# One core of a hybrid RWKV-7 / mLSTM / MoE block: the scheduler of the long stretch plans with mean durations from the trace

## The chip, the cores and the metric

The kernel runs on one core of a Trainium2 chip. The metric is the device time of one execution in microseconds (us). A core has five engines with their own instruction queues: TensorE (PE) for matmuls, VectorE (DVE), ScalarE (ACT), GpSimd (POOL), and SyncE (SP), which here only issues transfers (DMAs). A queue is worked off in order; an instruction whose inputs aren't there holds up all behind it on the same queue.

## What is computed

One block of an encoder on 1024 tokens of width 1024: a modulated RMS norm, one input projection, two groups of recurrent heads on its columns, an output projection, and a hierarchical mixture of experts. All of it is float32.

```python
# RWKV-7 group, 8 heads x 64: u is the projection's columns after the token shift
r, k, v, wd, ad, gd = split(u)
decay = exp(-exp(-softplus(-(w0 + tanh(wd) @ w_up)) - 0.5))
a = sigmoid(a0 + ad @ a_up);  g = sigmoid(gd) @ g_up
kk = normalise(k * k_k);  k = k * (1 + (a - 1) * k_a);  b = kk * a
state = state * decay_t + (state @ -kk_t) b_t + v_t k_t      # for each token t
y_t = state @ r_t                                            # then group norm, bonus, * g
# mLSTM group, 4 heads, qk 64 / v 128, in chunks, gated; then
x = x + gate * (concat(rwkv, mlstm) @ w_out)
x = x + gate * moe(rms_norm(x))        # top-1 of 4 groups, top-2 of 8 experts, 1024 -> 256 -> 1024
```

## The kernel before, in words

A product in full float32 precision is made from three passes of fp32r matmuls: the left and the right side are split into a high and a low part (hTh, hTl for the activations; whi, wlo for the weights), and high x high, low x high and high x low are added up. These matmuls, 128 rows by 512 columns, go into PSUM tiles named lane. A block of weights (wraw, five buffers, half of a 128-column block each) is fetched by SP, its high part is made on ACT, and its low part (wlo) on VectorE for one half and on POOL for the other (fetch_w, split_w).

The RWKV group is worked through in eight units, numbered 0 to 7: four pairs of heads in each half of 512 tokens. A unit has six parts, each a function. unit_prep makes decays, k, kk, AR and BK, mostly on VectorE; unit_rest makes what the scan needs besides; between them the products of AR and BK, masked to tiles G, are formed on TensorE and VectorE. unit_solve inverts 16 x 16 triangles: G is copied to DRAM (dF), read back turned (N), fifteen rounds of a multiplication (Xt) and a sum (XD) follow on VectorE, four writes put XD into DRAM (img), and two reads bring it back as D and X. unit_levels doubles the blocks to 32 and 64 with matmuls of D, G, X and T, beginning with tp<-D,G on TensorE and T<-tp,ll on VectorE. unit_scan goes through the chunks of the state (pr, pu, pp, py in PSUM; R, UV, st). unit_post is group norm, bonus and gate (nrs is its reciprocal square root, Y its result).

Beside the units stand: the remaining modulation vectors (ada_rest, 32 loads ada_w of 512 KB through three buffers, each followed by one scalar_tensor_tensor of 128 x 1024 on VectorE), the normalised input of the second half (xin, with its reciprocal square roots xrs and xss), the mLSTM gates and chunks (qko, vd, pB, rowd, yTd), and the lanes of the input and output projections.

From 63.8 us on the program isn't issued as it is written. A Recorder notes each operation with what it reads and writes (add), its step's priority (PRIO) and an expected duration (cost). flush then plans all of it with a list scheduler: it goes through planned time, and at each point gives every free engine the ready operation of the lowest rank, where rank is 20 x priority minus the longest planned path from the operation to the end (bl), if its tiles have space. The operations are issued in this order, for all five queues, up to 842.1 us. Every one is issued through the same line of add, so the profile puts all of them at L262 (L290 in the changed file). In cost, a matmul goes by its size, a VectorE operation takes 0.13 us + elements / 880, an ACT operation 0.2 + elements / 1350, a POOL operation 0.4 + elements / 610; in add, a DMA moves 300e3 bytes per us one after the other; in flush its result lands 1.7 us after that.

Of the kernel before, what the change touches and what calls it, by code (L numbers as in the profile page):

```python
# [9 lines left out]
F32R = mybir.dt.float32r  # L10
# [39 lines left out]
class View:  # L50
# [90 lines left out]
class Pool:  # L141


    def __init__(self, rec, make):
        self.rec, self.make, self.pool, self.users, self.opened = rec, make, None, [], None
        rec.control(self, True)

    def start(self):
# [42 lines left out]


PRIO = dict(prep=2, rest=3, lev=1, scan=0, post=4, gates=6, ada=9, rx=8, h=3, chunk=5, split=5, prod=7, fin=4, fetch=5, y=4)
PE_SLACK = 0.5
RANK = 20.0


class Recorder:
# [14 lines left out]
    def control(self, pool, begin):  # L213
        if self.mode != 'record':
            pool.start() if begin else pool.end()
            return
        o = Op()
        o.engine, o.what, o.cost, o.pe = 'ctl', None, 0.0, False
# [13 lines left out]
    def cost(self, engine, what, a, kw):  # L232
        free = lambda x: math.prod(x.shape[1:])
        if engine == 'tensor':
            out, w = a[0], a[1]
            n, m = free(out), free(w)
            if what == 'transpose':
                return 0.112
            if isinstance(w, View) and w.base.dtype_ == F32R:
                return 0.231 * max(n, 128) / 512  # L240
            if out.shape[0] <= 32:
                return 0.012 if n <= 32 else 0.05
            return 2 * max(0.112 * m / 128, 0.84e-3 * n, 0.05)
        out = a[0] if a else kw['out']
        n = max([free(x) for x in list(a) + list(kw.values()) if hasattr(x, 'shape')])
        if what.endswith('dma_start'):
            return 0.45
        if engine == 'vector':
            return 0.13 + n / 880.0 * (2 if what == 'tensor_tensor_scan' else 1)
        if engine == 'scalar':  # L250
            return 0.2 + n / 1350.0 + (0.19 if 'accum_out' in kw else 0)
        return 0.1 + n / 1500.0 if what == 'memset' else 0.4 + n / 610.0

    def add(self, engine, what, a, kw):
        o = Op()
        o.engine, o.what, o.pe = engine, what, engine == 'tensor'
        o.cost = self.cost(engine, what, a, kw)
        o.dma = 0.0
        if what.endswith('dma_start'):
            o.dma = 4.0 * math.prod(a[0].shape) / 300e3  # L260
        fn = getattr(self.nc, engine)
        call = lambda: getattr(fn, what)(*[real(x) for x in a], **{k: real(x) for k, x in kw.items()})  # L262
        writes = [a[0]] if a else [kw['out']]
        if 'accum_out' in kw:
            writes.append(kw['accum_out'])
# [3 lines left out]
        for x, w in acc:  # L269
            if isinstance(x, View):  # L270
                key, box = x.base, x.box
# [39 lines left out]
    def flush(self):  # L311
# [23 lines left out]
        free['ctl'] = 0.0  # L335
        dma_free = 0.0
        cand = {e: [] for e in free}
        for o in ops:
            if not o.wait:
                cand[o.engine].append(o)  # L340
        now, left = 0.0, len(ops)
        placed = set(t for s in self.slots.values() for t in s)
        self.plan = []
# [28 lines left out]
        while left:  # L372
            busy = False
            for e in free:
                if free[e] > now:
                    continue
                best = None
                for o in cand[e]:
                    if o.ready <= now:
                        if (best is None or (o.rank, o.seq) < (best.rank, best.seq)) and room(o, now):  # L380
                            best = o
                if best is None:
                    continue
                o = best
                busy = True
                cand[e].remove(o)
                left -= 1
                o.begin = now
                for t in o.tiles:
# [13 lines left out]
                for u in users[o]:  # L403
                    u.wait -= 1
                    lat = 0.0 if u.pe and o.pe else 0.1 if u.engine == o.engine or o.engine == 'ctl' else 0.15 + (PE_SLACK if u.pe else 0.0)
                    u.ready = max(u.ready, o.done + lat if not (u.pe and o.pe) else o.done)
                    if not u.wait:
                        cand[u.engine].append(u)
            if busy:
                continue  # L410
            nxt = [free[e] for e in free if free[e] > now]
# [15 lines left out]
class Block:  # L427
    def __init__(self, ctx, tc, aps):
# [4 lines left out]
        self.dram = ctx.enter_context(self.pool(name="dscr", bufs=1, space=DRAM))  # L433
        self.img = {}
        self.psum = ctx.enter_context(self.pool(name="psum", bufs=1, space=PSUM))

    def pool(self, **kw):
        return Pool(self.rec, lambda: self.tc.tile_pool(**kw))
# [2111 lines left out]
```

## Time and profile before

| | us |
|---|---|
| median of 3 runs | 1303.49 |
| lowest, highest | 1301.4, 1307.46 |
| the profiled execution | 1305.22 |
| its span (first to last instruction) | 1303.3 |
| mean granted TensorE clock, of full | 0.91 |
| the planned stretch | 63.8 to 842.1 |

The page gives busy time, share and count of each engine, then the span in 40 slices. In views by instruction, a row is start, duration, engine, line, operation, output<-inputs, shapes and how many there were in a row; in brackets stands how long the engine idled before and on what it waited. Groups give count, busy time and mean ns of one. SPq is SP's queue. Names lose their buffer numbers, so all eight units have the same ones and are told apart by time.

### The profile page before, as it was taken

How to read it: one execution, taken by the hardware profiler on the slowest of the kernel's cores; microseconds unless marked ns; L12 is line 12 of the kernel's file. 1: busy time of each engine (PE TensorE's matmuls, PEld its weight loads, DVE VectorE, ACT ScalarE, POOL GpSimd, SP SyncE). 2: the span in 40 equal slices, each digit the busy share in tenths (PEclk: the TensorE clock that was granted, in tenths of full speed). 3: DMA queues.
4: the chain of work that ended last, by engine and by line, in shares of the span. 5: the costliest groups of instructions: out<-in, count | busy, mean ns of one | idle time of the engine just before them, and what ended most of it. 6: DMA issues, size and time to landing. Idle time of an engine off the chain costs nothing.

```text
span 1303.3 us, 21771 instructions
## 1 busy us (share of the span) xinstructions
PE 1148.8 (88%) x7807; PEld 836.3 (64%) x7807; DVE 936.3 (72%) x2024; ACT 529.2 (41%) x1021; POOL 393.9 (30%) x464
## 2 busy tenths in 40 slices
PE   3886889797999999999898899995899999898893
PEld 3665666676676777776666677774666666565553
DVE  6699676876656878877748554834688888777766
ACT  5343112142433443333422333644455655455444
POOL 4623134221233242432133323543222222222112
PEclk8887677698999999999899699997799999999997
DMA  9525555475433443322433554699599999999974
GB/s 313 153 69 155 180 174 153 122 204 158 136 96 97 107 112 80 104 69 61 94 119 102 154 159 134 195 361 326 190 306 314 302 289 285 282 320 326 324 264 164
DMA packets 251935, 246.16 MB, mean 189 GB/s; under 512 B 55064, under 2 KB 190362, under 8 KB 251824
## 3 DMA queue, kind: packets, MB, share of 16 engines
q1 hardware_dynamic: 243504, 228.43, 56.2%
q0 software_dynamic: 8320, 16.31, 5.4%
q8 instruction: 62, 1.02, 0.3%
q14 instruction: 49, 0.40, 0.1%
HBM read 212.13 MB, written 44.74 MB: 197 GB/s over the span
## 4 chain that ended last, share of the span: by engine, by line
PE 62%; DMA 16%; DVE 13%; issue 3%; ACT 2%; SPq 1%; POOL 1%; DVEq 0%; ACTq 0%; POOLq 0%
PE lane L262 20%; PE tp L262 14%; PE yd L2049 8%; DMA wd<-in_moe_w_down_dram 4%; PE lane L787 4%; PE lane L788 4%; PE lane L789 3%; DMA ada_w<-in_ada_w_dram 2%; DMA D<-img 2%; DMA wa<-in_moe_w_gate_dram 2%; PE tp L2002 2%; PE lane L189 2%; PE py L262 1%; DMA X<-img 1%; DVE Xt L262 1%
## 5 line engine op out<-in xcount | busy, mean ns | idle before, releaser
L262 PE MATMUL lane<-hTh,whi 128*128 128x512 f32 (+1 forms) x469 | 213.5, 455 | 2.5 <-DVE v L262 0.7
L262 PE MATMUL lane<-hTl,whi 128*128 128x512 f32 (+1 forms) x469 | 192.3, 410 | 5.7 <-DVE hTl L262 5.7
L262 PE MATMUL lane<-hTh,wlo 128*128 128x512 f32 (+1 forms) x469 | 190.8, 407 | 3.1 <-DVE wlo L262 3.1
L262 ACT CAST whi<-wraw 128x512 fp32r<-128x512 f32 (+1 forms) x120 | 71.6, 607 | 163.8 <-PE lane L262 133.8
L2049 PE MATMUL yd<-wd,a 128*112 128x512 f32 x256 | 119.8, 607 | 12.5 <-DMA wd<-in_moe_w_down_dram 9.3
L262 POOL TENSOR_TENSOR wlo<-wraw,whi 128x512 fp32r<-128x512 f32 (+1 forms) x60 | 81.9, 1367 | 97.2 <-ACT whi L262 95.1
L262 PEld LDWEIGHTS lane<-hTh,whi 128*128 128x128 f32 (+1 forms) x469 | 91.0, 194 | 30.9 <-issue 2.2
L262 PEld LDWEIGHTS lane<-hTh,wlo 128*128 128x128 f32 (+1 forms) x469 | 90.9, 194 | 27.2 <-DVE wlo L262 4.8
L262 PEld LDWEIGHTS lane<-hTl,whi 128*128 128x128 f32 (+1 forms) x469 | 91.4, 195 | 20.6 <-DVE hTl L262 8.3
L1972 DVE TENSOR_TENSOR wl<-wa,wh 128x1024 fp32r<-128x1024 f32 x62 | 75.6, 1225 | 40.2 <-ACT wh L1971 38.8
L787 PE MATMUL lane<-wh,xh 128*112 128x512 f32 x256 | 103.9, 406 | 0.0
L788 PE MATMUL lane<-wl,xh 128*112 128x512 f32 x256 | 101.7, 397 | 0.0
L789 PE MATMUL lane<-wh,xl 128*112 128x512 f32 x256 | 100.7, 393 | 0.0
L262 POOL TENSOR_SCALAR sW<-st,WT 128x64 f32<-128x64 f32 x56 | 33.1, 592 | 215.5 <-DVE st L262 129.9
L2076 POOL DMA_INDIRECT x2d<-ys,idx x30 | 44.9, 1496 | 147.4 <-DVE ys L2060 138.5
L2049 PEld LDWEIGHTS yd<-wd,a 128*112 128x112 f32 x256 | 43.5, 182 | 65.4 <-issue 44.6
L1972 DVE TENSOR_TENSOR wl<-wb,wh 128x1024 fp32r<-128x1024 f32 x62 | 76.4, 1233 | 11.3 <-ACT wh L1971 9.6
L1971 ACT CAST wh<-wa 128x1024 fp32r<-128x1024 f32 x62 | 64.8, 1049 | 45.4 <-PE lane L789 36.5
L1971 ACT CAST wh<-wb 128x1024 fp32r<-128x1024 f32 x63 | 66.2, 1051 | 17.4 <-PE lane L789 8.3
L1978 POOL DMA_INDIRECT xt<-xad,idx x32 | 35.0, 1093 | 113.3 <-PE tp L2002 94.9
L262 DVE COPY UV<-pu 64x64 f32<-64x64 f32 x128 | 28.1, 220 | 38.3 <-PE pu L262 36.9
L789 PEld LDWEIGHTS lane<-wh,xl 128*112 128x112 f32 x256 | 44.9, 175 | 14.8 <-DVE xl L2015 0.4
(515 smaller groups left out, 2539.2 us busy)
## 6 DMA issues: line engine op xcount, KB each, us to landing
wd<-in_moe_w_down_dram SPq DMA_DIRECT2D x64, 512.0 KB
wraw<-in_w_in_dram SPq DMA_DIRECT2D x104, 256.0 KB
ada_w<-in_ada_w_dram SPq DMA_DIRECT2D x32, 512.0 KB
wa<-in_moe_w_gate_dram SPq DMA_DIRECT2D x32, 512.0 KB
wa<-in_moe_w_up_dram SPq DMA_DIRECT2D x32, 512.0 KB
wb<-in_moe_w_gate_dram SPq DMA_DIRECT2D x32, 512.0 KB
wb<-in_moe_w_up_dram SPq DMA_DIRECT2D x32, 512.0 KB
ada_w<-in_ada_w_dram SPq DMA_DIRECT2D x32, 256.0 KB
```

What stands on the lines that cost most here:

```text
L189: return getattr(eng, what)(*[real(x) for x in a], **{k: real(x) for k, x in kw.items()})
L262: call = lambda: getattr(fn, what)(*[real(x) for x in a], **{k: real(x) for k, x in kw.items()})
L787: nc.tensor.matmul(ps, l[0], r[0], start=first, stop=False)
L788: nc.tensor.matmul(ps, l[0], r[1], start=False, stop=False)
L789: self.mark = nc.tensor.matmul(ps, l[1], r[0], start=False, stop=last)
L1971: nc.scalar.copy(h, src)
L1972: (engs[n] if engs else nc.vector).tensor_tensor(l, src, h.bitcast(F32), op=ALU.subtract)
L1978: return self.nc.gpsimd.indirect_dma_start(out=self.xts[e % 3], out_offset=None, in_=self.xad[:], in_offset=bass.IndirectOffsetOnAxis(ap=s ...
L2002: self.nc.tensor.transpose(pt[:, j, :], v[:, j // 2, j % 2], self.ident[0:SL, 0:SL])
L2049: self.nc.tensor.matmul(y[:, b], a[:, i], d[:, i, b * 512:b * 512 + 512], start=(i == 0), stop=(i == 1))
L2076: self.nc.gpsimd.indirect_dma_start(out=self.x2d[:], out_offset=bass.IndirectOffsetOnAxis(ap=oi, axis=0), in_=ys, in_offset=None, bounds_c ...
```

## The change

The scheduler gets a table COST of mean durations in us, by engine (g, s, v), operation and the tag of the tile that is written. cost looks there first. What isn't in the table (matmuls, copies on ACT, tensor_reduce, and the tags R, UV, ada_rest among others) keeps the formula. The two DMA constants become 250e3 bytes per us and 2.0 us. The rest of the diff are hooks by which an operation could be put on another engine; other() gives None for all of them, so that alts stays empty.

```diff
+COST = {
...
+    ('v', 'tensor_tensor'): dict(nrs=0.2, wlo=0.85, BK=1.06, k=1.02, lg1=0.66, Xt=0.37, Y=0.76, hTl=0.97, msm=0.24, mrs=0.19),
...
+}
...
         if what.endswith('dma_start'):
             return 0.45
+        known = COST.get((engine[0], what), {}).get(out.base.key[1] if isinstance(out, View) else '')
+        if known:
+            return known
         if engine == 'vector':
...
+    def other(self, engine, what, a, kw):
+        return None
...
         if what.endswith('dma_start'):
-            o.dma = 4.0 * math.prod(a[0].shape) / 300e3
...
+            o.dma = 4.0 * math.prod(a[0].shape) / 250e3
+        o.alt = self.other(engine, what, a, kw)
...
-            o.bl = max((u.bl for u in users[o]), default=0.0) + o.cost + (0.25 if o.engine != 'ctl' else 0.0) + (getattr(o, 'dma', 0) and o.dma + 1.7)
+            o.bl = max((u.bl for u in users[o]), default=0.0) + o.cost + (0.25 if o.engine != 'ctl' else 0.0) + (getattr(o, 'dma', 0) and o.dma + 2.0)
...
-                for o in cand[e]:
+                for o in cand[e] + alts[e]:
                     if o.ready <= now:
-                        if (best is None or (o.rank, o.seq) < (best.rank, best.seq)) and room(o, now):
-                            best = o
+                        k = (o.rank, o.seq)
+                        if (best is None or k < key) and (o.engine == e or sooner(o, now)) and room(o, now):
+                            best, key = o, k
...
-                    o.done = max(dma_free, o.done + o.dma) + 1.7
+                    o.done = max(dma_free, o.done + o.dma) + 2.0
```

Every engine has as many instructions as before, in another order. Three places of it follow. The first is SP's queue in unit 6, from just after the first img write (img_586 is the DRAM image that XD is written to, D the tile that is read back from it). Before:

```order
L262 DMA wraw<-in_w_in_dram 128x4x128
L262 DMA img_586<-XD 16x32x16 x3
L262 DMA wraw<-in_w_in_dram 128x4x128 x2
L262 DMA vd<-vtm 128x4x128
L262 DMA D_6794<-img_586 128x1x256
```

The same place with the change:

```order
L290 DMA gn<-in_rwkv_gn_w_dram 128x128
L290 DMA img_586<-XD 16x32x16 x2
L290 DMA yTd<-yt 128x512
L290 DMA img_586<-XD 16x32x16
L290 DMA D_6761<-img_586 128x1x256
```

The loads of wraw and vd no longer stand between the writes of img and the read of D; the vector gn and yTd stand among the writes.

The second place is VectorE in unit 3, from the last G to the first Xt (N is the turned G, xin and xrs belong to the input of the second half, Y to the group norm of an earlier unit). Before:

```order
L262 TENSOR_TENSOR G_3016<-tp,mask 128x512
L262 TENSOR_TENSOR D_3070<-tp,D_2908 128x256
L262 SCALAR_TENSOR_TENSOR qko<-qks,qko 128x512
L262 STREAM_TRANSPOSE X<-D_3070 32x8x32 x4
L262 COPY bon<-tp 128x8
L262 COPY u_257<-lane 128x3
L262 TENSOR_SCALAR carry<-lane,pcol 128x1
L262 COPY UV_2856<-pu 64x64
L262 COPY UV_2861<-pu 64x64
L262 TENSOR_TENSOR Xt<-N_3119,XD 64x1
```

With the change 41 rows lie between the two; the first nine of them are:

```order
L290 TENSOR_TENSOR G_3279<-tp,mask 128x512
L290 COPY UV_2744<-pu 64x64
L290 COPY UV_2749<-pu 64x64
L290 TENSOR_TENSOR wlo<-wraw,whi 128x512
L290 COPY bon<-tp 128x8
L290 TENSOR_TENSOR Y<-Y,bv 128x512
L290 SCALAR_TENSOR_TENSOR st<-pp,WT,sW 128x64
L290 TENSOR_TENSOR Y<-Y,tp 128x512
L290 TENSOR_TENSOR R<-pr,AV 128x64
L290 COPY UV_2744<-pu 64x64
```

and the last five before the first Xt:

```order
L290 TENSOR_TENSOR xrs<-xrs,xss 128x1
L290 SCALAR_TENSOR_TENSOR xss<-xrs 128x1
L290 SCALAR_TENSOR_TENSOR xrs<-xrs 128x1
L290 TENSOR_SCALAR xin<-xin,xss 128x1024
L290 TENSOR_TENSOR Xt<-N_3381,XD 64x1
```

The four transposes of X went elsewhere, and steps of an earlier unit's scan and group norm and the chains of xrs, xss and xin came in.

The third place is SP's queue in unit 0, from the load of ada_rest's bias to the read of D (three rows of ada_w stand ahead of it in both). Before:

```order
L262 DMA ada_rest<-in_ada_b_dram 1x1024
L262 DMA img_586<-XD 16x32x16 x2
L262 DMA ada_w<-in_ada_w_dram 128x1024 x2
L262 DMA img_586<-XD 16x32x16
L262 DMA ada_w<-in_ada_w_dram 128x1024
L262 DMA img_586<-XD 16x32x16
L262 DMA ada_w<-in_ada_w_dram 128x1024
L262 DMA wraw<-in_w_in_dram 128x4x128 x2
L262 DMA D_1235<-img_586 128x1x256
```

With the change:

```order
L290 DMA ada_rest<-in_ada_b_dram 1x1024
L290 DMA wraw<-in_w_in_dram 128x4x128 x2
L290 DMA ada_w<-in_ada_w_dram 128x1024 x2
L290 DMA img_586<-XD 16x32x16
L290 DMA ada_w<-in_ada_w_dram 128x1024 x2
L290 DMA img_586<-XD 16x32x16
L290 DMA ada_w<-in_ada_w_dram 128x1024
L290 DMA img_586<-XD 16x32x16
L290 DMA ada_w<-in_ada_w_dram 128x1024
L290 DMA img_586<-XD 16x32x16
L290 DMA ada_w<-in_ada_w_dram 128x1024 x2
L290 DMA D_1201<-img_586 128x1x256
```

Eight loads of ada_w stand between the bias and D instead of four.

## Rows read from the trace of the kernel before

**Rows 1.** The page: busy us, share and instructions of each engine.

```profile
PE 1148.8 (88%) x7807; PEld 836.3 (64%) x7807; DVE 936.3 (72%) x2024; ACT 529.2 (41%) x1021; POOL 393.9 (30%) x464
PEclk8887677698999999999899699997799999999997
```

**Rows 2.** Table by stage; columns as its second line names them.

```profile
core 0: us, PE busy (x) PEld busy (x) DVE busy (x) ACT busy (x) POOL busy (x), PEclk, DMA share, GB/s
63.80:303.30 239.50, 197.49 (x1653) 150.47 (x1654) 191.12 (x423) 69.11 (x125) 67.06 (x76) 0.80 0.53 153
303.30:356.00 52.70, 50.71 (x498) 38.58 (x499) 33.42 (x122) 19.08 (x35) 8.35 (x13) 0.93 0.50 142
356.00:495.30 139.30, 133.60 (x1042) 99.07 (x1043) 96.84 (x265) 54.23 (x118) 47.36 (x66) 0.99 0.39 104
495.30:638.00 142.70, 134.46 (x1292) 97.21 (x1291) 112.71 (x312) 48.68 (x100) 42.57 (x64) 0.98 0.31 76
638.00:755.60 117.60, 104.72 (x791) 76.62 (x792) 69.56 (x196) 34.31 (x80) 39.33 (x43) 0.83 0.45 124
755.60:842.10 86.50, 83.41 (x627) 64.42 (x628) 52.50 (x144) 40.15 (x132) 34.78 (x40) 0.95 0.55 160
```

**Rows 3.** Timeline of TensorE, at full clock: start, duration, what.

```profile
223.57 0.39 PE L262 MATMUL lane<-hTh,whi 128*128 128x512 f32 x1
...
224.27 0.39 PE L262 MATMUL lane<-hTh,whi 128*128 128x512 f32 x1
...
397.16 0.66 PE L262 MATMUL tp<-ident,xin 128*128 128x128 f32 x4
397.58 0.50 PE L262 MATMUL lane<-hTh,whi 128*128 128x512 f32 x1
...
399.22 0.34 PE L262 MATMUL pp<-UV,BKT 128*64 128x64 f32 x4
```

**Rows 4.** Groups on VectorE, 67 to 842 us: count, busy us, mean ns, idle before.

```profile
L262 DVE SCALAR_TENSOR_TENSOR ada_rest<-ada_w,csil,ada_rest 128x1024 f32<-128x1024 f32 x32 | 42.4, 1324 | 4.1 <-DMA ada_w<-in_ada_w_dram 4.0
...
L262 DVE SCALAR_TENSOR_TENSOR nrs<-nrs 128x8 f32<-128x8 f32 x80 | 17.0, 229 | 1.1
...
L262 DVE TENSOR_TENSOR BK<-k,Ei 64x512 f32<-64x512 f32 x16 | 14.6, 910 | 0.2
...
L262 DVE TENSOR_TENSOR k<-k,aa 128x512 f32<-128x512 f32 x8 | 8.2, 1022 | 0.0
```

**Rows 5.** Timeline of VectorE in unit 3's chain.

```profile
308.12 0.69 DVE L262 TENSOR_TENSOR G<-tp,mask 128x512 f32<-128x512 f32 x1 [3.10 <-PE tp L262]
...
318.59 0.46 DVE L262 COPY UV<-pu 64x64 f32<-64x64 f32 x2 [3.67 <-PE pu L262]
319.08 0.15 DVE L262 TENSOR_TENSOR Xt<-N,XD 64x1 f32<-64x1 f32 x1
...
331.49 0.38 DVE L262 TENSOR_REDUCE XD<-Xt 64x15 f32<-64x225 f32 x1
...
356.04 0.42 DVE L262 TENSOR_TENSOR T<-tp,ll 128x256 f32<-128x256 f32 x1 [1.32 <-PE tp L262]
```

**Rows 6.** Timeline of SP's queue in unit 6, from the last img writes to D.

```profile
619.12 1.56 SPq L262 DMA_DIRECT2D img<-XD  x3
626.62 3.35 SPq L262 DMA_DIRECT2D wraw<-in_w_in_dram  x2
...
631.02 0.54 SPq L262 DMA_DIRECT2D D<-img  x1
```

**Rows 7.** Timeline of TensorE at the same place.

```profile
636.89 1.08 PE L262 MATMUL tp<-D,G 32*32 32x32 f32 x64 [4.46 <-DMA D<-img]
```

**Rows 8.** Timeline of VectorE: one operation at two times.

```profile
121.14 1.74 DVE L262 TENSOR_TENSOR k<-k,aa 128x512 f32<-128x512 f32 x1
...
247.78 0.68 DVE L262 TENSOR_TENSOR k<-k,aa 128x512 f32<-128x512 f32 x1
```

**Rows 9.** Waits of TensorE, 67 to 842 us: total us, times, longest.

```profile
PE tp L262 <- DMA D<-img: 17.6, 6, 5.8
```

**Rows 10.** Waits of SP's queue, 67 to 842 us.

```profile
SPq L262 <- POOL wlo L262: 70.8, 23, 6.6
```

More of the change, by code (lines that the diff above doesn't have):

```diff
@@ L144, in __init__ @@
     def __init__(self, rec, make):
-        self.rec, self.make, self.pool, self.users, self.opened = rec, make, None, [], None
+        self.rec, self.make, self.pool, self.users, self.opened, self.psum = rec, make, None, [], None, False
         rec.control(self, True)
@@ L193 @@
 PRIO = dict(prep=2, rest=3, lev=1, scan=0, post=4, gates=6, ada=9, rx=8, h=3, chunk=5, split=5, prod=7, fin=4, fetch=5, y=4)
+COST = {
+    ('g', 'memset'): dict(X=0.52, cs=0.52, adr=0.95),
+    ('g', 'tensor_copy'): dict(WT=0.49, XD=0.69),
+    ('g', 'tensor_scalar'): dict(sW=0.59, gd=0.62, qko=1.02, mnv0=0.73),
+    ('g', 'tensor_tensor'): dict(AR=1.39, wlo=1.37, BK=1.58, bv=1.32, k=0.32, wdad=0.19, r=0.55, v=0.34, gd=0.19, hTl=1.39, qko=1.3),
+    ('s', 'activation'): dict(cs=0.72, sw=0.65, aa=0.69, Wp=0.63, gt=0.68, lg0=0.63, lg1=0.63, k=0.69, row_lf=0.63, lg2=0.63, gd=0.65, r=0.68, qko=0.43, qks=0.63, v=0.68, y2=0.63, junk=1.06, hTh=0.78, wdad=0.66, pB=0.37),
+    ('v', 'reciprocal'): dict(lg0=3.34),
+    ('v', 'scalar_tensor_tensor'): dict(nrs=0.23, nrm=0.29, qko=0.63, st=0.28, stf0=0.28, stf1=0.28, xrs=0.18, xss=0.17, stf2=0.27, pB=0.39, stf3=0.28, mC=0.34, mrs=0.18),
+    ('v', 'tensor_copy'): dict(row_mp=0.22),
+    ('v', 'tensor_scalar'): dict(sw=0.42, nrs=0.21, gt=0.41, lg1=0.42, lg2=0.42, row_lf=0.41, carry=0.21, gvr=0.32, xin=0.75, hv=0.81, msm=0.24, mrs=0.18),
+    ('v', 'tensor_tensor'): dict(nrs=0.2, wlo=0.85, BK=1.06, k=1.02, lg1=0.66, Xt=0.37, Y=0.76, hTl=0.97, msm=0.24, mrs=0.19),
+    ('v', 'tensor_tensor_scan'): dict(cs=1.25, row_b=1.21),
+}
 PE_SLACK = 0.5
 RANK = 20.0
+FLEX = 512
 class Recorder:
@@ L217, in control @@
         o = Op()
-        o.engine, o.what, o.cost, o.pe = 'ctl', None, 0.0, False
+        o.engine, o.what, o.cost, o.pe, o.alt = 'ctl', None, 0.0, False, None
         o.run = pool.start if begin else pool.end
@@ L258, in add, with call @@
         o.dma = 0.0
+        o.f32r = o.pe and a[1].base.dtype_ == F32R
         if what.endswith('dma_start'):
-            o.dma = 4.0 * math.prod(a[0].shape) / 300e3
-        fn = getattr(self.nc, engine)
-        call = lambda: getattr(fn, what)(*[real(x) for x in a], **{k: real(x) for k, x in kw.items()})
+            o.dma = 4.0 * math.prod(a[0].shape) / 250e3
+        o.alt = self.other(engine, what, a, kw)
+        o.home = engine
+        def call():
+            e = getattr(self.nc, o.engine)
+            if o.engine != o.home and callable(o.alt[1]):
+                return o.alt[1](e, *[real(x) for x in a])
+            return getattr(e, what if o.engine == o.home else o.alt[1])(*[real(x) for x in a], **{k: real(x) for k, x in kw.items()})
         writes = [a[0]] if a else [kw['out']]
@@ L337, in flush, with sooner @@
         cand = {e: [] for e in free}
+        alts = {e: [] for e in free}
+        def sooner(o, now):
+            t = max(free[o.engine], now) + o.cost
+            for x in cand[o.engine]:
+                if x is not o and x.ready <= now and (x.rank, x.seq) < (o.rank, o.seq):
+                    t += x.cost
+            return now + o.alt[2] < t
         for o in ops:
@@ L340, in flush @@
                 cand[o.engine].append(o)
+                if o.alt:
+                    alts[o.alt[0]].append(o)
         now, left = 0.0, len(ops)
@@ L385, in flush @@
                 busy = True
-                cand[e].remove(o)
+                cand[o.engine].remove(o)
+                if o.alt:
+                    alts[o.alt[0]].remove(o)
+                    if o.engine != e:
+                        o.engine, o.cost = e, o.alt[2]
                 left -= 1
```

3 lines of the change are left out of this document (added).

## The prediction

> **What bounds the kernel now.** I read the page first, for engines and clock. TensorE counts as busy for 88% of the span and VectorE for 72%, with the TensorE clock below full in places [rows 1], so no engine is simply full. The edit only reaches the stretch from 63.8 to 842.1 us, which the list scheduler orders; before and after it the code is the same. The second view is therefore the table by stage [rows 2]. I cut the stretch where VectorE makes T of units 2, 3, 4, 6 and 7 (numbered from 0), because there each unit's solve chain ends: matmuls, G, the copies dF and N, fifteen rounds of Xt and XD on VectorE, four writes of img, reads of D and X, the first levels on TensorE, T. The eight chains are serial, and the program puts other work beside them.
>
> I priced every instruction of the stretch once. On TensorE a 512-column lane matmul follows the last by 0.23 us (three in 0.70), a 128-column fp32 transpose takes 0.105 (four in 0.42) and a small product of the state under 0.1 (four in 0.34) [rows 3]; VectorE goes by the means of its groups, as [rows 4] shows for four of them. The sums are about 572 us for TensorE and 598 us for VectorE in 778 us of stretch, equal in both kernels, as the instructions and their engines are. About 200 us are thus waits between engines, latency, and time at the lower clock level, and a new order can only change those. By stage, priced TensorE / priced VectorE / real: I (63.8 to 303.3) 155 / 207 / 239.5; II (to 356.0) 41 / 37 / 52.7; III (to 495.3) 117 / 107 / 139.3; IV (to 638.0) 115 / 123 / 142.7; V (to 755.6) 79 / 78 / 117.6; VI 64 / 47 / 86.5. In I VectorE is the bound: 1.16 us real per priced us. In III it is TensorE: 1.19, at a granted clock of 0.99 [rows 2]. In V the clock is 0.83 and neither engine is full: latency.
>
> **What the change costs by itself.** The table and the two DMA constants are read when the kernel is built; no instruction is added or changes engine, and the hooks for another engine always get None. That part is zero. In the plan a 512 KB load now lands 0.65 us later (0.35 for the rate, 0.3 for the latency) and k takes 1.02 us instead of 0.71, so that what depends on them is placed later. What is left is the order, counted at the same marks in the two orders (priced as above).
>
> Stage I: VectorE 207 → 196, TensorE 155 → 161 (33 lane matmuls more). What leaves VectorE here is mainly one unit's preparation (aa, k, kk, AR, three BK: about 7 us) and a group-norm chain with its Y steps (sixteen small nrs operations, some 0.23 each, and four of about 0.8), against one more wlo [rows 4]. At 1.16 that is −13. Against it: for unit 0 the order now puts eleven loads of ada_w instead of seven between N and the read of D (the third pair of order rows). A load needs one of three buffers, so D stands behind the eighth ada_rest step instead of the fourth: 4 × 1.32 us [rows 4] = 5.3. The ends are 0, if VectorE, which does these steps anyway, stays the bound, and 5.3 if the chain is; I take 3, the middle, and 2 for the six added TensorE us. Stage I: **−8**.
>
> Stage II: TensorE 41 → 57. Of this 18 us instead of 2 stand before unit 3's first G (36 lane matmuls × 0.23 = 8.3, 29 transposes × 0.105 = 3.0, 46 small products × 0.09 = 4). At the stage's own ratio 52.7/41 = 1.28 that is 18 × 1.28 = 23, in place of the 4.8 us from 303.3 to the first G at 308.1 [rows 5]. Then the chain: before, G to T took 47.9 us (308.1 to 356.0), of it 11.0 to the first Xt and 12.8 for the rounds to 331.9 [rows 5]. Now a reciprocal-square-root chain, two scalings of xin and a Y step stand on VectorE between the last G and the first Xt (the second pair of order rows): about 10 us by their means, of which some was waiting before (VectorE stood 3.67 us for a TensorE result in it [rows 5]). I take +8, between 0 and 10. New stage: 23 + 56 = 79 against 52.7: **+26**.
>
> Stage III: TensorE 117 → 96, 60 lane matmuls less, VectorE 107 → 96. At 1.19: −21 × 1.19 = **−25**.
>
> Stage IV: TensorE −4 us × 1.24 (142.7/115) = −5. At unit 6 the read of D now follows its last img write directly, where two loads of wraw and one of vd stood between (the first pair of order rows). Before, SP had issued the last three img writes by 620.7, then stood until 626.6 for the first of these loads and gave D at 631.0 [rows 6]; TensorE, out of other work, waited 4.46 us for it [rows 7]. D can come about 6.5 us earlier. But TensorE has only 26 priced us of other work left over the chain instead of 33: 4.46 + 7 − 6.5 = 5 us of waiting again, so nothing is won at the place where the queue is relieved. I take **−2**, half of the −5, as these are not lane-bound us alone.
>
> Stages V and VI: +6 priced us in V, where neither engine is full and unit 7's chain has 3 us more of cover: **+2**; −2 × 1.34 in VI: **−3**.
>
> Sum: −8 + 26 − 25 − 2 + 2 − 3 = −10. The profiled execution took 1305.2 us (span 1303.3) and lies 1.7 above the median of the runs shown, 1303.5; so 1295 against it and **1294 us** against the median.
>
> **What speaks against measured means.** The same operation on the same shape took 1.74 us at 121.1 and 0.68 at 247.8 [rows 8]; the table gives every such k one price, 1.02, which neither was. Means are better than the old formula (0.71) only where a price belongs to the kind and not to its neighbours. The Trainium skill, "SBUF — State Buffer", section "Who interferes with whom", has VectorE and GpSimd share a port pair as an exclusive lock: a VectorE operation with two inputs in SBUF and a GpSimd operation that reads SBUF block each other. By that rule the prices follow the order and the new order makes new ones; the trace agrees so far as 1.74 against 0.68 goes, and the time would be the second rival's below.
>
> **Rivals.** *(a) Slower: the work drawn ahead of unit 3 isn't repaid.* Place: 18 us of TensorE work before unit 3's first G. For: every chain after it is serial, so a later G moves all later ones. It decides if stage III is bound by unit 4's own chain and not by TensorE: then III gives back only the issue time of its 60 lane matmuls, 60 × 0.23 = 14, not 25, and stages I, IV, V and VI give nothing. 26 − 14 = +12, about **1316 us**. Against: clock 0.99 and 133.6 of 139.3 us busy in III [rows 2].
>
> *(b) Same: the orders are two draws of one lot.* The plan models TensorE and its waits as it did; SP stood 70.8 us for POOL's wlo [rows 10], and the same loads stand in the new order's queue at other places; my own terms of +26 and −25 cancel to a us. Time within 6.5 us of before, say **1303 us**.
>
> *(c) Faster: the queue's relief counts in full.* TensorE waits 17.6 us in 6 places for D behind img [rows 9]. If at units 4, 5 and 6, where the order takes wraw, vd, yTd or qod out from between img and D, the chain shortens by 5 us each (a little over the 4.46 us that TensorE stood at unit 6 [rows 7]), and these chains are the path, then −10 − 15 = −25, **1279 us**. Against: the cover argument of stage IV.
>
> *(d) The change doesn't reach the order.* The orders differ on every engine, so nothing for it.
>
> **How the numbers follow.** About 0.5% (6.5 us) is what a measurement of this kernel tells from no change. Forecast 0.32 (centre 1294, own range 1287 to 1300: its part above 1297 counts as same), (a) 0.24, (b) 0.28, (c) 0.16. Faster is (c) and 0.27 of the forecast, 0.43; same is (b) and the forecast's upper part 0.05, less 0.01 for the side of slower, 0.32; slower is (a) with that, 0.25. The range runs from below (c)'s centre to just above (a)'s: 1277 to 1317. It holds the unknown ends (0 to 5.3 for unit 0's D, 0 to 10 for unit 3's chain, 25 or 14 in III) and leaves out the near half of (c) below, 0.07, and of (a) above, 0.11.
>
> **What would show it.** T of unit 2 should be 8 us earlier, about 295; T of unit 3 some 18 us later, about 374; T of unit 4 about 488, 7 us earlier; the stretch should end about 832. Unit 3's G to T should be 56 us, unit 6's D should issue right after its last img write, and the wait of TensorE for D should stay near 17 us. If T of unit 4 is late, (a) holds; if the wait for D falls by 10 us or more and the end with it, (c). The forecast is wrong above all if stage II's +26 and stage III's −25, two large terms from the same moved work, do not cancel.

## The result, and the profile after

The changed kernel took 1347.5 us (median of 4 runs, 1345.4 to 1351.0) against 1302.5 us for the kernel before in the same comparison: ratio 1.035, 95% interval 1.0301 to 1.040, so slower by 45 us. The profiled execution took 1347.0 us; its span of 1345.1 us is 41.8 longer than that of before. The page of the changed kernel, engines and clock, to be read against [rows 1]:

```profile
PE 1168.2 (87%) x7807; PEld 844.1 (63%) x7807; DVE 922.7 (69%) x2024; ACT 529.0 (39%) x1021; POOL 394.6 (29%) x464
PEclk8987868999799788899897589979699999999897
```

The counts are those of before. TensorE is busy 19 us longer with the same instructions, VectorE 14 us less.

The table by stage, cut at the same marks (T of units 2, 3, 4, 6 and 7, then a place just behind the planned stretch, now at 878.4 us), columns as in [rows 2]. This last mark, 842.1 us before, is not quite the end of the stretch, though it was called that: the last planned TensorE instruction ends at 835.4 us before and at 869.8 now.

```profile
63.80:295.90 232.10, 196.29 (x1662) 147.52 (x1662) 177.57 (x395) 70.08 (x128) 64.40 (x75) 0.85 0.55 158
295.90:376.40 80.50, 73.15 (x663) 54.52 (x663) 57.45 (x185) 26.00 (x50) 21.44 (x27) 0.89 0.44 124
376.40:504.50 128.10, 115.48 (x867) 84.41 (x867) 84.30 (x228) 46.94 (x97) 34.97 (x47) 0.92 0.33 85
504.50:660.00 155.50, 137.85 (x1279) 100.47 (x1279) 104.94 (x316) 44.09 (x97) 43.31 (x67) 0.91 0.29 74
660.00:792.00 132.00, 114.12 (x816) 84.09 (x816) 70.16 (x209) 38.63 (x96) 42.66 (x49) 0.81 0.44 117
792.00:878.40 86.40, 81.67 (x615) 61.97 (x616) 50.08 (x127) 38.26 (x121) 34.84 (x38) 0.95 0.54 157
```

| stage | before, us | after, us | difference | forecast | TensorE idle before → after (length less busy) |
|---|---|---|---|---|---|
| I | 239.5 | 232.1 | −7.4 | −8 | 42.0 → 35.8 |
| II | 52.7 | 80.5 | +27.8 | +26 | 2.0 → 7.4 |
| III | 139.3 | 128.1 | −11.2 | −25 | 5.7 → 12.6 |
| IV | 142.7 | 155.5 | +12.8 | −2 | 8.2 → 17.7 |
| V | 117.6 | 132.0 | +14.4 | +2 | 12.9 → 17.9 |
| VI | 86.5 | 86.4 | −0.1 | −3 | 3.1 → 4.7 |
| after the last mark | 461.2 | 466.7 | +5.5 | 0 | |

The first two stages came out as forecast. The loss behind them is in III to V, where −25 was forecast and +16.0 came: there TensorE stands idle 21.4 us longer (26.8 → 48.2), and the granted clock is 0.92, 0.91 and 0.81 where it was 0.99, 0.98 and 0.83. With its two levels of 1.0 and 0.5 that makes some 97 us at the lower level in these three stages, against 49. In stage IV TensorE has less work than before by the count (−4 priced us) and is busy 3.4 us longer.

What TensorE waits for, from the view of waits from 67 to 878 us (total us, times, longest), to be read against [rows 9]:

```profile
PE tp L290 <- DVE BK L290: 9.2, 1, 9.2
...
PE tp L290 <- DVE Y L290: 8.5, 1, 8.5
...
PE tp L290 <- DMA D<-img: 4.7, 3, 3.5
```

The wait for D fell from 17.6 to 4.7 us. The longest new wait, 9.2 us for BK, lies in stage I and the one for Y in stage IV. Summed over all rows of this view up to the last planned TensorE instruction, TensorE's waits for DMAs fell from 21.8 to 5.1 us, those for VectorE rose from 36.3 to 62.4 and those for ACT from 5.5 to 18.0.

Unit 6 shows in one place how a gain turned into another wait. SP's queue there (compare [rows 6]):

```profile
643.10 0.95 SPq L290 DMA_DIRECT2D img<-XD  x2
649.38 0.34 SPq L290 DMA_DIRECT2D yTd<-yt  x1
649.76 0.43 SPq L290 DMA_DIRECT2D img<-XD  x1
652.05 0.54 SPq L290 DMA_DIRECT2D D<-img  x1
```

D leaves 1.9 us after the last write of img, as forecast. TensorE at the same place (compare [rows 7]):

```profile
638.02 1.05 PE L290 MATMUL tp<-gu,gd 128*128 128x128 f32 x8
...
647.56 1.11 PE L290 MATMUL tp<-ident,Y 128*128 128x128 f32 x4 [8.49 <-DVE Y L290]
649.15 0.76 PE L290 MATMUL lane<-hTh,whi 128*128 128x512 f32 x1 [0.47 <-DVE v L290]
...
659.20 0.75 PE L290 MATMUL tp<-D,G 32*32 32x32 f32 x64
```

The levels (tp<-D,G) no longer wait for D. But ahead of the lane matmuls that are to fill the time stand the transposes of unit 5's group norm Y, and TensorE waited 8.49 us for Y. (The first of these lane matmuls waits 0.47 us more, for v, which VectorE makes behind Y, so it could not have run much earlier in this order either.) VectorE made this Y between the rounds of unit 6's Xt and XD, and then put a reciprocal of the mLSTM gates before its last step:

```profile
640.70 0.37 DVE L290 TENSOR_REDUCE XD<-Xt 64x15 f32<-64x225 f32 x1
641.00 0.67 DVE L290 TENSOR_TENSOR Y<-Y,gn 128x512 f32<-128x512 f32 x1
...
642.72 0.69 DVE L290 TENSOR_TENSOR Y<-Y,bv 128x512 f32<-128x512 f32 x1
643.45 3.34 DVE L290 RECIPROCAL lg<-lg 4x512 f32<-4x512 f32 x1
646.82 0.69 DVE L290 TENSOR_TENSOR Y<-Y,tp 128x512 f32<-128x512 f32 x1
```

Before, 4.46 us were waited for D here; now 8.49 for Y. Idle time costs a second time through the clock: behind the wait for Y the granted clock is at its lower level, 0.50, for 6 us, and lane matmuls of the same size start 0.42 us apart instead of 0.23. (Before, the clock stood at 0.50 for some 7 us behind the wait for D, mostly past the mark in stage V; this place thus lost 4 us of waiting and nothing more by the clock.) The stretch at the lower level and the next one, columns as above, and lane matmuls of each:

```profile
647.50:653.60 6.10, 5.57 (x19) 4.51 (x20) 4.50 (x6) 1.24 (x3) 0.00 (x0) 0.50 0.20 53
653.60:660.00 6.40, 6.35 (x116) 4.88 (x114) 5.59 (x12) 4.38 (x9) 2.80 (x5) 1.00 0.28 81
```

```profile
649.71 0.63 PE L290 MATMUL lane<-hTl,whi 128*128 128x512 f32 x1
650.13 0.63 PE L290 MATMUL lane<-hTh,wlo 128*128 128x512 f32 x1
...
653.94 0.39 PE L290 MATMUL lane<-hTl,whi 128*128 128x512 f32 x1
654.17 0.39 PE L290 MATMUL lane<-hTh,wlo 128*128 128x512 f32 x1
```

Unit 3's chain, the second place shown (compare [rows 5]):

```profile
317.76 2.62 DVE L290 TENSOR_TENSOR G<-tp,mask 128x512 f32<-128x512 f32 x4
...
335.63 1.21 DVE L290 TENSOR_TENSOR Xt<-N,XD 64x1 f32<-64x1 f32 x1
...
351.23 0.38 DVE L290 TENSOR_REDUCE XD<-Xt 64x15 f32<-64x225 f32 x1
...
376.42 0.42 DVE L290 TENSOR_TENSOR T<-tp,ll 128x256 f32<-128x256 f32 x1 [1.82 <-PE tp L290]
```

The first G comes 21.9 us after T of unit 2 (forecast 23), and from G to T it is 58.7 us (forecast 56).

### The profile page after: what moved, and what is told of

The parts are those of the page before. It is cut to its first block, busy times and chain, and to the rows that moved or that the text cites. A ratio compares the mean times of both kernels' runs of the same rounds, so it can differ in the third digit from the quotient of the medians.

```text
span 1345.1 us, 21758 instructions
## 1 busy us (share of the span) xinstructions
PE 1168.2 (87%) x7807; PEld 844.1 (63%) x7807; DVE 922.7 (69%) x2024; ACT 529.0 (39%) x1021; POOL 394.6 (29%) x464
## 4 chain that ended last, share of the span: by engine, by line
PE 63%; DMA 16%; DVE 13%; issue 3%; ACT 2%; POOL 1%; SPq 1%; DVEq 0%; POOLq 0%; ACTq 0%
PE lane L290 22%; PE tp L290 13%; PE yd L2097 7%; PE lane L189 3%; PE lane L836 3%; PE lane L835 3%; PE lane L837 3%; DMA wd<-in_moe_w_down_dram 3%; DMA ada_w<-in_ada_w_dram 2%; DMA wa<-in_moe_w_gate_dram 2%; PE tp L2050 2%; DVE ada_rest L290 1%; PE py L290 1%; DMA X<-img 1%; DVE Xt L290 1%
## 5 line engine op out<-in xcount | busy, mean ns | idle before, releaser
L290 PE MATMUL lane<-hTh,whi 128*128 128x512 f32 (+1 forms) x469 | 218.9, 467 | 11.3 <-ACT hTh L290 4.9
L290 PE MATMUL lane<-hTh,wlo 128*128 128x512 f32 (+1 forms) x469 | 195.0, 416 | 4.0 <-DVE wlo L290 4.0
L290 PE MATMUL lane<-hTl,whi 128*128 128x512 f32 (+1 forms) x469 | 195.8, 417 | 1.6 <-DVE hTl L290 1.5
L2097 PE MATMUL yd<-wd,a 128*112 128x512 f32 x256 | 123.4, 624 | 11.4 <-DMA wd<-in_moe_w_down_dram 7.6
L290 POOL TENSOR_SCALAR sW<-st,WT 128x64 f32<-128x64 f32 x56 | 38.9, 696 | 182.4 <-DVE st L290 109.5
L290 DVE TENSOR_TENSOR wlo<-wraw,whi 128x512 fp32r<-128x512 f32 (+1 forms) x60 | 52.0, 871 | 8.8 <-ACT whi L290 8.3
L2108 DVE SCALAR_TENSOR_TENSOR ys<-yd,tb,gf 112x512 f32<-112x512 f32 x64 | 45.0, 745 | 15.4 <-PE yd L2097 15.4
```

Of the source, the lines that this page charges most:

```text
L290: return getattr(e, what if o.engine == o.home else o.alt[1])(*[real(x) for x in a], **{k: real(x) for k, x in kw.items()})
L2097: self.nc.tensor.matmul(y[:, b], a[:, i], d[:, i, b * 512:b * 512 + 512], start=(i == 0), stop=(i == 1))
L2108: nc.vector.scalar_tensor_tensor(ys[:, bs], py[b], cw, self.gf[0:SL, bs], op0=ALU.mult, op1=ALU.mult)
```

## The experiments

All orders were run beside the kernel before. The stretch in this table goes from the first to the last planned TensorE instruction of the profiled execution; idle is its length less TensorE's busy time; IV is the time from T of unit 4 to T of unit 6; VectorE's planned sum is what the scheduler reckons with. In the diffs, `...` marks what is left out.

| run | VectorE planned, us | median, us | ratio, 95% interval | stretch | busy | idle | IV |
|---|---|---|---|---|---|---|---|
| before | 522 | 1301 to 1304 | 1 | 771.7 | 698.1 | 73.5 | 143 |
| the change | 600 | 1347.5 | 1.030 to 1.040 | 806.0 | 712.3 | 93.6 | 156 |
| e1 table only | 600 | 1345.9 | 1.028 to 1.035 | 812.5 | 707.8 | 104.7 | 164 |
| e2 DMA constants only | 522 | 1337.2 | 1.022 to 1.027 | 801.0 | 706.1 | 94.9 | 158 |
| e3 before, factors 1 | 522 | 1328.2 | 1.016 to 1.024 | 786.3 | 701.6 | 84.7 | 145 |
| e4 before, factors 2 | 522 | 1307.7 | 1.001 to 1.007 | 776.6 | 694.5 | 82.1 | 135 |
| e5 old, then new | 522, then as 600 | 1339.4 | 1.023 to 1.037 | 803.0 | 706.9 | 96.1 | 156 |
| e6 new, then old | 600, then as 522 | 1315.5 | 1.007 to 1.020 | 784.4 | 698.4 | 86.1 | 142 |
| e7 the change, factors 1 | 600 | 1347.4 | 1.028 to 1.040 | 814.0 | 715.0 | 99.0 | 168 |
| e8 before, factors 3 | 522 | 1319.1 | 1.009 to 1.021 | 784.2 | 706.2 | 78.0 | 160 |
| e9 the change, TensorE × 1.12 | 600 | 1342.1 | 1.023 to 1.034 | 809.8 | 722.1 | 87.7 | 168 |
| e10 VectorE rows only | 600 | 1345.8 | 1.027 to 1.039 | 816.4 | 715.1 | 101.3 | 185 |
| e11 ACT rows only | 522 | 1320.6 | 1.005 to 1.019 | 786.0 | 710.9 | 75.1 | 147 |
| e12 the change without Xt | 582 | 1342.4 | 1.027 to 1.038 | 800.6 | 696.5 | 104.2 | 168 |
| e13 before, VectorE × 1.15 | 600 | 1333.0 | 1.014 to 1.028 | 798.6 | 710.5 | 88.1 | 154 |
| e14 the change, VectorE × 0.87 | 522 | 1323.2 | 1.011 to 1.024 | 782.5 | 699.3 | 83.2 | 151 |
| e15 before, VectorE × 0.87 | 454 | 1315.6 | 1.005 to 1.017 | 776.5 | 689.8 | 86.7 | 165 |
| e16 before, tight rounds | 522 | 1350.4 | 1.030 to 1.043 | 819.3 | 712.0 | 107.3 | 155 |
| e17 e13 with factors 2 | 600 | 1353.0 | 1.029 to 1.043 | 816.9 | 705.2 | 111.8 | 155 |
| e18 e14 with factors 2 | 522 | 1329.5 | 1.011 to 1.026 | 794.4 | 703.5 | 90.8 | 151 |

### Which part, and how much any disturbance costs

e1 takes the DMA constants back, e2 takes the table away:

```diff
 # e1
-            o.dma = 4.0 * math.prod(a[0].shape) / 250e3
+            o.dma = 4.0 * math.prod(a[0].shape) / 300e3
...
-            o.bl = ... + (getattr(o, 'dma', 0) and o.dma + 2.0)
+            o.bl = ... + (getattr(o, 'dma', 0) and o.dma + 1.7)
...
-                    o.done = max(dma_free, o.done + o.dma) + 2.0
+                    o.done = max(dma_free, o.done + o.dma) + 1.7
 # e2
-        known = COST.get((engine[0], what), {}).get(...)
+        known = COST.get((engine[0], what) if engine[0] in 'x' else '', {}).get(...)
```

> The table COST as in the changed kernel, with the old DMA constants (300e3 bytes per us, 1.7 us). Theory A (the table does it: with dearer VectorE operations the plan puts other VectorE work into the serial solve chains): about 1345, within 10 us of the changed kernel's 1347.5. Theory B (the order is a draw: before happens to have a good one, and any change of the numbers loses some tens of us): anything from 1310 to 1360. Theory C (the DMA constants do it): 1300 to 1310, as before.

> Only the DMA constants of the change (250e3 bytes per us, 2.0 us), with the old formula for every duration. A: within 8 us of before, 1302. B: 1310 to 1345, as any other change of the numbers. C: about 1345.

e3, e4 and later e8 leave the kernel before as it is but for factors without meaning:

```diff
         o.cost = self.cost(engine, what, a, kw)
+        if self.mode == 'record' and engine not in ('tensor', 'sync'):
+            o.cost *= 1 + 0.05 * (((len(self.ops) * 7919 + 1237) % 101) / 50.0 - 1)   # e4: 2474, e8: 3711
```

> The kernel before, with the planned cost of every operation off TensorE and SP multiplied by a fixed factor between 0.95 and 1.05 that differs from operation to operation, without meaning. A: within 8 us of before, on either side. B: slower by 10 us or more, 1312 to 1345. C: as A.

> As e3_before_pert1 with another set of factors between 0.95 and 1.05. A: within 8 us of before, 1294 to 1310. B: slower by 10 us or more, 1312 to 1345, and by another amount than e3_before_pert1. C: as A.

> A third set of factors on the kernel before. If before's order is a lucky draw among its neighbours: slower by 4 to 30 us as with the first two, 1307 to 1335. If the first two were chance: 1290 to 1305, as likely faster as slower.

The table alone costs 42 us, the DMA constants alone 33, both together 45: the parts don't add up. The factors cost 25, 4 and 16 us (ratios 1.0195, 1.0037, 1.015). So theory A, that the table alone does it, falls (e2 and e3 lie far outside its 8 us, though e1 came out as it said and e4 lies inside). Theory C, that the DMA constants do it, falls by e1. Theory B, that before has a good draw of an order, holds in so far as every neighbour of before's order was slower; e4, at a ratio of 1.0037, hardly, and by less than the 10 us that B asked for. It isn't the whole answer, as the next run shows, which puts the factors of e3 on the changed kernel:

> The changed kernel with the factors of e3_before_pert1 (0.95 to 1.05 on every planned cost off TensorE and SP). If orders are draws and the table shifts their centre by nothing: like the disturbed orders of before, 1305 to 1340, below the changed kernel's 1347. If the table shifts the centre: 1335 to 1365.

It took 1347.4 us, and the orders with the table (1346, 1347) lie above all three disturbed ones of before (1308 to 1328), which points to a shift of the centre on top of the scatter.

### Where the time goes: one set of numbers up to unit 3's T, the other behind it

e5 and e6 keep both durations of each operation, and change from one to the other at a point of planned time, so that the order ahead of it is that of one kernel. In the traces VectorE, ACT and POOL work in before's order up to 362 us in e5, and in the changed kernel's up to 385 us in e6 (c and d are the two costs of each operation, noted in add and flush):

```diff
+        def rules(k):
+            for o in reversed(ops):
+                if o.begin is None:
+                    o.cost, o.dma = o.c[k], o.d[k]
+                o.bl = max((u.bl for u in users[o]), default=0.0) + o.c[k] + (0.25 if o.engine != 'ctl' else 0.0) + (o.d[k] and o.d[k] + (1.7, 2.0)[k])
+                o.rank = RANK * o.prio - o.bl
+        rules(0)               # e6: 1
...
         while left:
+            if now >= 246.5 and self.rules == 0:      # e6: 288.6, from 1
+                rules(1)
```

> The scheduler plans with the old numbers until unit 3's T, so that the order up to there is that of before, and from there on with the changed ones. Theory M (the work moved ahead of unit 3 isn't repaid, rival a): nothing is moved ahead here, so within 10 us of before, 1294 to 1312. Theory S (the orders that the changed numbers give after unit 3 lose by themselves): stages III to VI lose as in the changed kernel, 13 + 14 + some of III, 1325 to 1350.

> The reverse: the changed numbers until unit 3's T, so that the order up to there is that of the changed kernel, T of unit 3 at 376 us instead of 356, then the old numbers. M: the 20 us lost by unit 3's T stay, 1320 to 1335. S: the old rules give the moved work back as the forecast had it (-25 in stage III), 1294 to 1308.

e5 took 1339.4 us, e6 1315.5. Stages III, IV and V of e5 and then of e6, columns as above:

```profile
358.90:502.80 143.90, 130.57 (x1026) 97.44 (x1025) 96.42 (x259) 53.50 (x113) 48.68 (x66) 0.95 0.39 100
502.80:658.90 156.10, 133.20 (x1296) 95.78 (x1295) 110.19 (x320) 47.42 (x103) 40.38 (x62) 0.92 0.27 66
658.90:791.40 132.50, 118.52 (x819) 86.08 (x820) 70.12 (x210) 38.97 (x95) 40.90 (x47) 0.83 0.43 118
```

```profile
372.70:502.10 129.40, 115.75 (x893) 84.85 (x890) 82.66 (x234) 47.06 (x105) 37.86 (x54) 0.93 0.37 96
502.10:644.30 142.20, 132.91 (x1261) 93.70 (x1261) 111.16 (x302) 48.24 (x96) 44.15 (x63) 0.97 0.29 71
644.30:767.30 123.00, 105.91 (x801) 78.28 (x800) 67.16 (x200) 33.72 (x86) 35.91 (x42) 0.82 0.45 117
```

With nothing moved ahead of unit 3, the new numbers still lose 13.4 us in IV (156.1 against 142.7) and 14.9 in V, as much as the changed kernel; with the changed kernel's first half, the old numbers bring IV back to 142.2. Theory S (the orders that the new numbers give behind unit 3 lose by themselves) holds for IV and V: with one and the same order up to there, the numbers used behind it make 38 us (before and e5) and 32 us (e6 and the change). Theory M (the work moved ahead isn't repaid) is not shown: e6 ends 14 us late, over S's 1294 to 1308 and under M's 1320 to 1335. Its T of unit 3 is 16.8 us late, its T of unit 4 only 6.8, and 5.4 are lost anew in V. These 14 us are also within what the meaningless factors cost, and the 38 and 14 do not add up to 45.

### Is it VectorE's price, and its level or its kinds?

e10 and e11 take one engine's rows of the table, with the old DMA constants; e9 raises TensorE's planned costs; e12 drops one entry:

```diff
 # e10 ('v'), e11 ('s')
-        known = COST.get((engine[0], what), {}).get(...)
+        known = COST.get((engine[0], what) if engine[0] in 'v' else '', {}).get(...)
 # e9
-        o.cost = self.cost(engine, what, a, kw)
+        o.cost = self.cost(engine, what, a, kw) * (1.12 if o.pe and self.mode == 'record' else 1.0)
 # e12
-    ('v', 'tensor_tensor'): dict(..., lg1=0.66, Xt=0.37, Y=0.76, ...),
+    ('v', 'tensor_tensor'): dict(..., lg1=0.66, Y=0.76, ...),
```

> Only the VectorE rows of the table, old DMA constants. P: these rows alone make VectorE the plan's bound, 1335 to 1355. D: as any other draw, 1305 to 1350.

> Only the ACT rows of the table, old DMA constants; the planned sums of TensorE and VectorE stay those of before. P: like the disturbed orders of before, 1300 to 1325. D: the same or up to 1350.

> The changed kernel with every planned TensorE cost of the stretch times 1.12, the inverse of the clock granted there (0.88 to 0.90). Summed over the stretch the plan held 586 us of TensorE and 522 of VectorE before; the table makes VectorE 600, so that the plan takes VectorE for the bound where the trace has TensorE busy 698 and VectorE 550. Theory P (the shift comes from raising one side of this ratio alone): with 656 against 600 the time falls to 1300 to 1322. Theory D (the orders are draws with no such centre): 1325 to 1360.

> The changed kernel without the entry Xt=0.37, which prices all fifteen rounds of a solve chain alike where the trace has 0.15 to 0.55 us. Theory X (the flat price lets other VectorE work into the chains: 198 operations between the rounds instead of 148, rounds 157 us in all instead of 134): the rounds go back to 134 to 140 us in all and the time to 1320 to 1330. P and D: 1335 to 1355.

The VectorE rows alone give the whole loss (1345.8), the ACT rows one like the disturbed orders' (1320.6). The POOL rows were not run alone. e9 stayed at 1342.1: theory P, that raising VectorE's side of the ratio to TensorE does it, falls, since 656 planned us of TensorE against 600 of VectorE did not bring the time back. e12 (1342.4) lies in the range of P and of D, that the orders are mere draws. Theory X, that the flat price of Xt lengthens the rounds, asked for rounds of 134 to 140 us in all; they went back from 157 to 147 only, and the time hardly moved. e16 below tests X by itself.

e13 to e15, then e17 and e18 as a repeat with factors 2, take level and kinds apart. The edit is the same line with another factor or the other kernel; e17 and e18 have the factors of e4 besides:

```diff
-        o.cost = self.cost(engine, what, a, kw)
+        o.cost = self.cost(engine, what, a, kw) * (1.15 if engine == 'vector' and self.mode == 'record' else 1.0)
 # e13, e17: before, 1.15;  e14, e18: the changed kernel, 0.87;  e15: before, 0.87
```

> The kernel before with every planned VectorE cost times 1.15: the planned sum of VectorE is that of the changed kernel, 600 us instead of 522, but the kinds keep the old formula's proportions and nothing else changes. Theory L (the level of VectorE's prices against TensorE's does it): 1333 to 1355, like every order planned with the VectorE rows. Theory K (the kinds' own prices do it): 1305 to 1330, like the disturbed orders of before.

> The changed kernel with every planned VectorE cost times 0.87: the kinds keep the table's proportions, the planned sum is again 522 us. L: 1305 to 1330. K: 1333 to 1355.

> The kernel before with every planned VectorE cost times 0.87 (454 us in all). L: cheaper VectorE gives no loss of the kind, 1295 to 1325, perhaps below before. If any change of level loses, whichever its sign: 1330 to 1350.

> The kernel before with the factors of e4_before_pert2 (which alone cost 4 us) and every planned VectorE cost times 1.15. Theory L (the level of VectorE's prices loses some 25 us by itself): 1325 to 1345. If e13 was only another draw: 1303 to 1322.

> The changed kernel with the same factors and every planned VectorE cost times 0.87. L: 1308 to 1330, as e14. If e14 was only another draw of orders whose centre is the changed kernel's: 1335 to 1355.

The level without the kinds: 1333.0 and 1353.0. The kinds without the level: 1323.2 and 1329.5. Cheaper VectorE: 1315.6, no better than before. e13 lies on the lower edge of L's range and e17 above it; e14 and e18 lie in it. Over all orders planned with VectorE at about 600 us (or 582 in e12, or from unit 3 on in e5) the times are 1333 to 1353; with 522 or less they are 1303 to 1330, but for e2 and e16, which change planned latencies. This points to the level for most of the shift, with the kinds' own proportions, at the old level, as good or bad as any disturbance. It isn't shown beyond that: there are two orders of each sort, the nearest of them (e13 with 1333.0, e18 with 1329.5) are 3.5 us apart with intervals that overlap, e2 and e16 are slow without any change of level, and one sort of meaningless factors alone makes 4 to 25 us.

Neither level is VectorE's own. In before's trace the durations of the 1436 planned VectorE operations add up to 607 us, but VectorE is busy with them for 548 us: in its records the next operation starts before the last has ended in 783 places, by 0.075 us in the mean, as Y at 641.00 above starts before XD ends at 641.07. Mean durations count this overlap twice, so the table's 600 us is 9% above the busy time, where the formula's 522 is 5% below it. No order was planned at the level of 548.

### Shorter chains

e16 leaves the kernel before but for one latency of the plan:

```diff
-                    lat = 0.0 if u.pe and o.pe else 0.1 if u.engine == o.engine ...
+                    lat = 0.0 if u.pe and o.pe else 0.0 if o.engine == u.engine == 'vector' and o.tiles and u.tiles and any(t.key[1] in ('Xt', 'XD') for t in o.tiles if t in u.tiles) else 0.1 if u.engine == o.engine ...
```

> The kernel before with one latency of the plan changed: between the Xt and XD of one solve chain the plan puts 0 instead of 0.1 us, so that no other VectorE operation fits between the rounds. Theory X (interleaved rounds lengthen the serial chains): rounds from X to X in all eight units 134 us fall to 80 to 95 us, as the rounds' own busy time is 72, and the time falls by 10 to 35 us, to 1270 to 1295. If the rounds are covered by TensorE work, or the gain is a draw's size: 1300 to 1325.

Unit 3's rounds on VectorE and its T, then the whole stretch:

```profile
339.97 0.16 DVE L262 TENSOR_TENSOR Xt<-N,XD 64x9 f32<-64x9 f32 x1
...
348.83 0.38 DVE L262 TENSOR_REDUCE XD<-Xt 64x15 f32<-64x225 f32 x1
...
374.62 0.42 DVE L262 TENSOR_TENSOR T<-tp,ll 128x256 f32<-128x256 f32 x1 [2.37 <-PE tp L262]
```

```profile
63.70:883.00 819.30, 712.02 (x5867) 531.50 (x5864) 557.72 (x1441) 261.36 (x582) 227.75 (x295) 0.87 0.42 118
```

The rounds did what was expected: about 9 us a unit, 74 us in all instead of 134. From the last G to T the eight chains now take 314 us in all instead of 384, and the kernel is 49 us slower, outside both ranges that were expected. The 70 us, and 48 more, reappear between the chains, from one unit's T to the next one's G, and behind the last T: stage VI is 111 us against 80 in the same measure. TensorE is idle 107 us instead of 73.5. Theory X falls with it, and so does the notion that these chains are the path: over the twenty orders their sum does not go with the time (374 us in e17 at 1353.0, 435 in e18 at 1329.5).

## Why the prediction was wrong

It gave 1294 us with a range of 1277 to 1317; the measured 1347.5 lies 30 us above the range and on the other side of no change.

*Stages I and II* were right: −7.4 for −8, +27.8 for +26. The counts of the two orders, the prices from the groups [rows 4] and the ends for unit 0's D and unit 3's chain hold where VectorE is the bound (it is busy 13.5 us less in I) or where one known batch of work stands before one known wait. Luck had a part in both. In I, T of unit 0 came 5.5 us later (137.7 to 143.2), the whole of the term for D and not its middle, T of unit 1 came 19.7 later (203.1 to 222.8), and only unit 2 brought the −7.4. In II, TensorE was busy 21.3 of the 21.8 us before unit 3's first G, at a granted clock of 1.00: more work stood there than the 18 priced us, and it did not run at the ratio of 1.28 that made 23 of them.

*Stage III, −25, is the first step that failed.* It multiplied 21 priced us by 1.19, the stage's real time by its priced time in the order before. Busy time did fall by 18.1 us (133.6 to 115.5), but idle time rose by 6.9. The ratio isn't a property of the stage: it holds the idle time and the clock of one order. Neither came out as before: TensorE took 1.20 us busy per priced us (115.5 for 96) at a granted clock of 0.92, where it took 1.14 at 0.99, so that busy time fell by some 6 us less than 21 × 1.14; and idle time did not shrink with the work, it grew.

*Stages IV and V, −2 and +2, are the larger failure:* +12.8 and +14.4. They were priced by the difference of work alone, as though the order inside the stage were neutral. Of the +27, 14.4 are TensorE idle, and the rest is TensorE busy longer, 12.8 for 2 more priced us; the granted clock fell from 0.98 to 0.91 in IV and from 0.83 to 0.81 in V, a cost that no term of the sum held. (V of before had been read as latency, with neither engine full; TensorE was busy there for 104.7 of 117.6 us, at a granted clock of 0.83.) e5 shows that the loss doesn't come from the stages ahead, and e10 that the VectorE rows suffice. At unit 6 the step "nothing is won where the queue is relieved" was right in its result and wrong in its reason: no wait for D came back, another wait in TensorE's own queue took its place (8.49 us for 4.46). (By the 1.9 us from the last write to D, the D of before could have come 8.4 us earlier, not 6.5.) How the rest of the loss in IV and V divides among single waits was not followed.

*The tail* was put at 0 and gave +5.5 us behind the last mark, +7.5 behind the last planned TensorE instruction (467.9 to 475.4). By the second measure e1, e5 and e10, nearly as slow as the change, have tails within 3 us of before's, so it isn't needed for the loss; over the twenty orders it goes from 464.3 to 475.4 with the same code, and why is not known.

*Rival (a)* was right in sign. Its price for the moved work, +12 and 1316 us, is what e6 measured (1315.5), but by another way, as half of e6's loss arises in V; its stage III (−14) is nearer to −11.2 than the forecast's −25. It has no part of the other 30 us. *Rival (c)* had its mechanism come true (17.6 → 4.7 us of waiting for D) and its time not. *Rival (b)* had the right name and the wrong size. Two orders of one lot were given ±6.5 us, in part on the ground that two of my own terms cancelled. Factors of 5% cost 4, 16 and 25 us; that scatter, which no view of one profile shows, should have set the width of the range, and all of it lay on the slow side.

*Behind all of it* stood the premise that the eight serial chains are the path. Summed over the stretch the chains, from the last G to T, are 384 us before and 419 after, which fits the result; but in e1 they are 389 at 42 us slower, and in e16 314 at 49 us slower. What went with the time is how well TensorE's queue is filled: 73.5 us idle in before is the least of all twenty orders (75 to 112 in the others), with 690 to 722 us busy for the same instructions. That says where the time lies and not what puts it there.

*What stays open.* Why a higher level of VectorE's prices leads this scheduler to worse orders. The ratio to TensorE isn't it (e9). A longer planned path also weighs more against the fixed 20 us of a priority step in the rank; that wasn't tried. Whether it is the level at all, and not draws, is argued from four orders (e13, e14, e17, e18). That before's numbers had been chosen for the order they give would explain why all neighbours lose; it is argued, not shown.

## What to carry to other kernels

Durations nearer to the trace in a greedy list scheduler do not mean a better order: the plan changes everywhere, and here each such change of the plan cost time. And mean durations that overlap add up to more than the engine is busy. Before trusting a forecast of such a change, disturb the numbers by a few per cent without meaning and time that; the scatter (here 4 to 25 us of 1303) is the least that an order's time is uncertain by. A stage's idle time isn't proportional to its work, and in this kernel a chain that got shorter (e16) gained nothing, as the fullest engine stood idle longer for it.

## What the runs showed of the hardware

A VectorE operation of one element per partition stood until the GpSimd operation beside it was done. In the changed kernel the first Xt of unit 3 (335.63, 1.21 us, shown above) ended at 336.84 with POOL's wlo at 336.83; without POOL at work the same form took 0.15. In e16 it happens again inside the rounds, at a form that took 0.20 at 628.94 of the changed kernel. POOL of the changed kernel, then VectorE of the changed kernel in unit 6, then POOL and VectorE of e16:

```profile
335.12 1.71 POOL L290 TENSOR_TENSOR wlo<-wraw,whi 128x512 fp32r<-128x512 f32 x1
```

```profile
624.24 0.15 DVE L290 TENSOR_TENSOR Xt<-N,XD 64x1 f32<-64x1 f32 x1 [0.83 <-DMA N<-dF]
```

```profile
341.09 1.29 POOL L262 TENSOR_TENSOR wlo<-wraw,whi 128x512 fp32r<-128x512 f32 x1 [1.38 <-ACT whi L262]
```

```profile
341.19 1.26 DVE L262 TENSOR_TENSOR Xt<-N,XD 64x36 f32<-64x36 f32 x1
```

The Trainium skill, "SBUF — State Buffer", section "Who interferes with whom", says that a VectorE instruction with two inputs in SBUF contends with a GpSimd instruction that reads SBUF, and calls the shared port pair an exclusive lock. The two pairs above agree: the VectorE operation, which starts second, ends within 0.1 us of the POOL operation. So does the whole stretch of before: all 55 planned tensor_tensor operations of VectorE that took over 0.3 us more than the shortest of their kind and form overlap a POOL operation (of all 553, 200 do), and their excess sums to 44 us. This excess moves with the neighbours that an order gives, and a table of means spreads it over all of the kind.
